# First pair of features of each FFN by eight plain products 512 wide, with the sums of blocks of x made beside it

## The chip, the cores and the metric

The kernel runs on 1 core of one Trainium2 chip. The metric is the device time of one execution in microseconds, the median of the runs shown; lower is better.

## What is computed

Two layers, each an FFN, a mixer and a second FFN, over 512 tokens (S) of 1024 features (DM). The change lies in the FFN alone; it runs four times (ffn1 and ffn2 of two layers).

```python
def rms_norm(x, w):
    xf = x.astype(jnp.float32)
    y = xf * lax.rsqrt(jnp.mean(xf * xf, axis=-1, keepdims=True) + NORM_EPS)
    return (y * w.astype(jnp.float32)).astype(x.dtype)

def swiglu_ffn(x, w_gate, w_up, w_down):
    return (jax.nn.silu(x @ w_gate) * (x @ w_up)) @ w_down

    for l in range(DEPTH):
        x = x + 0.5 * swiglu_ffn(rms_norm(x, ffn1_norm_w[l]), ffn1_w_gate[l], ffn1_w_up[l], ffn1_w_down[l])
        x = x + hybrid_mixer(rms_norm(x, mix_norm_w[l]), l, ...)
        x = x + 0.5 * swiglu_ffn(rms_norm(x, ffn2_norm_w[l]), ffn2_w_gate[l], ffn2_w_up[l], ffn2_w_down[l])
```

D_FF is 2816: 22 blocks of 128 features, worked on as 11 pairs (p = 0 to 10).

## The kernel before, in words

x lies in SBUF as eight tiles `x0` to `x7`, [128 features, 512 tokens] each. All arithmetic is fp32. A product of two fp32 operands is made of three matmuls: each operand is split into a rounded part (hi) and the rest (lo), and `mm3` (L114) issues hi·hi (L115), hi·lo (L116 or L117, by which operand has the lo part) and lo·hi. For weights `split` (L105) makes `whi` on ScalarE (L110) and `wlo` on VectorE (L111).

**Pairs.** `gate_up(p)` (L310) makes gate and up (s = 0, 1) of two feature blocks for all tokens. It sees weights and x as 2 x 2 block matrices (two feature blocks by odd and even input blocks; left and right half of the tokens, 256 each) and uses seven products of blocks and sums of blocks in place of eight. `STEPS` names the seven, in their order:

```python
    STEPS = (("11", 0, "X"), ("s1", 3, "Y"), ("s2", 4, "X"), ("s4", 2, "Y"), ("s3", 5, "X"), ("12", 1, "Z"), ("22", 6, "X"))
```

A product is 2 (s) x 4 (k) x 3 matmuls, 256 wide: 168 for a pair. Weights of a step are one tile [128, 1024], 512 KB. "11", "12", "21" and "22" are blocks as they lie in memory; s1 = 21 + 22, s2 = 11 - s1 with VectorE (L324), s4 = 12 + s2, s3 = 11 - 21. In most pairs s1 and s4 are made by accumulating DMAs on POOL's queue (L239, L326). A "plain" pair, p = 0 of each FFN and p = 1 of the first FFN, instead loads four `raw` blocks and makes s1 and s4 on VectorE too (L319). `raw` tiles (four buffers, shared with all other weights) are loaded by `load` (L98, L103), `rx` tiles (six buffers) by `loadx` (L223); both loads are on SP's queue, which takes them in order and stands where a buffer isn't free. The seven products are added into `c` by ScalarE and VectorE (L342 to L350), `c` is multiplied by the row `rsb` of 1/rms (L356), and silu(gate)·up is split into `hh`, `hl`.

**x for an FFN.** The blocks and sums of blocks of x, with their lo parts (`xR0` to `xR2`, `xT`), are made before the FFN begins: by `prep7` (L143) each time two tiles of x are finished, in w_out of the mixer (L1009) or in the last part of `down` (L374), and by `prep_all` (L249) at the start of the first FFN. `prep` (L129), which makes plain `xh`, `xl` of a tile, serves the mixer only. Squares of x are added into `sqacc` (L126). For the FFN `rms` (L302) multiplies `sqacc` by a matrix of ones (512 wide, L306) after the fifth product of pair 0, and `rstd` works on the 128x512 result; for the mixer `rms_of_x` (L187) makes four columns by eight one-column matmuls (L190), `rstd` works on 128x4, and `spread` (L195) makes the row.

**Order.** The instructions are written for one engine after the other as the code runs; a scheduler interleaves them by priority (`tc.high_priority()` puts loads and splits as early as buffers allow) and each engine then works strictly in its order. `after(n)` (L386) puts side work behind product n of a pair: rms, the bias row of the attention (`build_bias`, L416, in pair 1 of the first FFN: a load, two matmuls L426 through the single `side` bank, two copies L427, a store) and pieces of `down`.

## Time and profile before

| | us |
|---|---|
| median of 3 runs | 2014.24 (2011.62 to 2016.08) |
| the profiled execution | 2018.65 |
| its span | 2016.5 |

The profile and the trace are of one execution. Engines: PE is TensorE (PEld its weight loads), DVE VectorE, ACT ScalarE, POOL GpSimd, SP the engine that issues most DMAs (SPq its queue). L115 is line 115 of the kernel. Busy times are sums over an engine's instructions; an instruction that waits isn't busy. Matmuls overlap one another, so the step from start to start, and not the length of one, tells how fast they follow; VectorE's instructions overlap a little too. In brackets at the end of a row of the timeline stands how long the engine was idle before it and what released it. Consecutive like instructions stand in one row, with "x3" for three of them. PEclk is the TensorE clock that was granted, 1.00 being full speed.

### The profile page before, as it was taken

How to read it: one execution, taken by the hardware profiler on the slowest of the kernel's cores; microseconds unless marked ns; L12 is line 12 of the kernel's file. 1: busy time of each engine (PE TensorE's matmuls, PEld its weight loads, DVE VectorE, ACT ScalarE, POOL GpSimd, SP SyncE). 2: the span in 40 equal slices, each digit the busy share in tenths (PEclk: the TensorE clock that was granted, in tenths of full speed). 3: DMA queues.
4: the chain of work that ended last, by engine and by line, in shares of the span. 5: the costliest groups of instructions: out<-in, count | busy, mean ns of one | idle time of the engine just before them, and what ended most of it. 6: DMA issues, size and time to landing. Idle time of an engine off the chain costs nothing. (4 is left out here: it accounts for less than half of the span.)

```text
span 2016.5 us, 32318 instructions
## 1 busy us (share of the span) xinstructions
PE 1941.6 (96%) x12766; PEld 1761.9 (87%) x12766; DVE 1446.8 (72%) x2207; ACT 991.9 (49%) x1732; POOL 117.5 (6%) x173
## 2 busy tenths in 40 slices
PE   5899999999999899999989999999999988999999
PEld 5799999888878799999879999998898778999997
DVE  7876675769667697667679676657787687867665
ACT  6444443546545454444455454435466454545442
POOL 0100000011000000000000000000200000000000
PEclk8899999999989999999989999999999999999999
DMA  3766652445432675654257656525554127665622
GB/s 137 234 174 178 168 146 74 143 141 155 119 83 68 181 219 154 178 154 124 71 162 198 184 162 170 139 66 153 158 146 128 51 69 234 186 176 158 176 79 84
DMA packets 100099, 291.50 MB, mean 145 GB/s; under 512 B 10647, under 2 KB 23223, under 8 KB 99948
## 3 DMA queue, kind: packets, MB, share of 16 engines
q1 hardware_dynamic: 81900, 228.29, 34.5%
q0 software_dynamic: 18048, 61.15, 15.7%
q8 instruction: 100, 1.64, 0.3%
q14 instruction: 51, 0.42, 0.1%
HBM read 256.31 MB, written 7.66 MB: 131 GB/s over the span
## 5 line engine op out<-in xcount | busy, mean ns | idle before, releaser
L110 ACT CAST whi<-raw 128x1024 fp32r<-128x1024 f32 (+3 forms) x293 | 269.8, 921 | 443.2 <-PE side L116 221.5
L111 DVE TENSOR_TENSOR wlo<-raw,whi 128x1024 fp32r<-128x1024 f32 (+3 forms) x293 | 311.4, 1063 | 119.7 <-ACT whi L110 118.6
L115 PE MATMUL acc<-xT,whi 128*128 128x256 f32 x816 | 232.8, 285 | 0.8 <-ACT c L344 0.5
L116 PE MATMUL acc<-xT,whi 128*128 128x256 f32 x816 | 231.8, 284 | 0.0
L117 PE MATMUL acc<-xT,wlo 128*128 128x256 f32 x816 | 230.9, 284 | 0.1
L115 PE MATMUL side<-hh,whi 128*128 128x512 f32 x576 | 229.2, 398 | 0.0
L117 PE MATMUL side<-hh,wlo 128*128 128x512 f32 x576 | 226.9, 394 | 0.0
L116 PE MATMUL side<-hl,whi 128*128 128x512 f32 x576 | 225.8, 392 | 0.0
L117 PE MATMUL aux<-xR,wlo 128*128 128x256 f32 x704 | 201.3, 286 | 9.9 <-DVE wlo L111 9.9
L115 PE MATMUL aux<-xR,whi 128*128 128x256 f32 x704 | 203.0, 288 | 7.1 <-ACT whi L110 7.1
L116 PE MATMUL aux<-xR,whi 128*128 128x256 f32 x704 | 201.0, 285 | 0.0
L110 ACT CAST whi<-rx 128x1024 fp32r<-128x1024 f32 x117 | 122.6, 1048 | 140.1 <-PE aux L116 71.3
L111 DVE TENSOR_TENSOR wlo<-rx,whi 128x1024 fp32r<-128x1024 f32 x117 | 143.1, 1223 | 61.4 <-ACT whi L110 61.4
L115 PEld LDWEIGHTS acc<-xT,whi 128*128 128x128 f32 x816 | 157.8, 193 | 4.8 <-ACT c L344 1.6
L374 DVE TENSOR_TENSOR x<-side,x 128x512 f32<-128x512 f32 x96 | 66.3, 690 | 132.5 <-PE side L117 132.4
L111 DVE TENSOR_TENSOR wlo<-s,whi 128x1024 fp32r<-128x1024 f32 x98 | 119.4, 1223 | 58.4 <-ACT whi L110 58.1
L116 PEld LDWEIGHTS acc<-xT,whi 128*128 128x128 f32 x816 | 157.7, 193 | 2.0
L117 PEld LDWEIGHTS acc<-xT,wlo 128*128 128x128 f32 x816 | 156.6, 192 | 0.5 <-DVE wlo L111 0.5
L117 PEld LDWEIGHTS aux<-xR,wlo 128*128 128x128 f32 x704 | 136.7, 194 | 10.6 <-DVE wlo L111 10.6
L115 PEld LDWEIGHTS aux<-xR,whi 128*128 128x128 f32 x704 | 137.0, 195 | 9.9 <-ACT whi L110 7.3
L110 ACT CAST whi<-s 128x1024 fp32r<-128x1024 f32 x98 | 102.5, 1048 | 76.5 <-PE acc L116 26.7
L116 PEld LDWEIGHTS aux<-xR,whi 128*128 128x128 f32 x704 | 137.1, 195 | 2.0 <-issue 1.0
(351 smaller groups left out, 5037.2 us busy)
## 6 DMA issues: line engine op xcount, KB each, us to landing
rx<-wgu SPq DMA_DIRECT2D x156, 512.0 KB, 4.7
raw<-wgu SPq DMA_DIRECT2D x98, 512.0 KB, 4.6
raw<-wd SPq DMA_DIRECT2D x96, 384.0 KB, 3.3
rx<-wgu POOLq DMA_DIRECT2D x39, 512.0 KB, 7.6
rx<-s POOLq DMA_DIRECT2D x39, 512.0 KB, 6.4
raw<-win SPq DMA_DIRECT2D x24, 512.0 KB, 4.6
raw<-winf SPq DMA_DIRECT2D x24, 512.0 KB, 3.6
raw<-wd SPq DMA_DIRECT2D x32, 256.0 KB, 2.7
```

What stands on the lines that cost most here:

```text
L110: act.copy(hi[:, :n], raw[:, lo:lo + n])
L111: eng.tensor_tensor(lw[:, :n], raw[:, lo:lo + n], hi[:, :n].bitcast(F32), ALU.subtract)
L115: pe.matmul(out, lh, rh, start=first, stop=False, skip_group_check=skip)
L116: pe.matmul(out, lh, rl, start=False, stop=False, skip_group_check=skip)
L117: pe.matmul(out, ll, rh, start=False, stop=last, skip_group_check=skip)
L374: dve.tensor_tensor(x[d], ps, x[d], ALU.add)
```

## The change

Pair 0 of each FFN is no longer made by seven products of sums but by `gate_up0`: its four weight blocks times plain `xh`, `xl`, 2 x 4 x 3 matmuls for each, 96 in all, 512 wide. The first two blocks come as `raw`, the last two as `rx`. Its results are multiplied out of PSUM by `rsb` (four VectorE operations, 512 wide). So x is handed to each FFN as to the mixer, by `prep` for one tile at a time (with the first FFN the tiles come even ones first, behind two blocks of weights), and `prep7` and `prep_all` are gone. The sums of blocks of x are made behind the products of pair 0 (`sums(0)` to `sums(2)`) and behind the first product of pair 1 (`last_sum`), 256 wide, into three tiles and into parts of `xh`, `xl` that pair 0 has done with. rms goes through four columns behind product 0 and is spread behind product 2. Pair 1 of the first FFN is made like the later pairs, with accumulating DMAs. The bias row's inputs are loaded in pair 0, its matmuls come in pair 2 (before, pair 1), and its copies to 128 partitions in pairs 5 to 8 (before, 3 to 6).

```diff
-    def prep7(i, wcol, tmp, four):
...
-    def sums(t, b, out, eng):
...
-        def plain(p):
-            return p == 0 or first and p == 1
...
-            if plain(p):
-                return {b: load(w[n], soon) for n, b in ((0, "11"), (2, "21"), (3, "22"), (1, "12"))
-                        if not (first and p == 0 and n == 0)}
-            r = {"11": loadx(w[0]), "s1": loadx(w[2])}
-
-            with tc.high_priority():
+            r = {"11": loadx(w[0], soon), "s1": loadx(w[2], soon)}
+
+            with tc.high_priority() if soon else nullcontext():
                 pool.dma_start(out=r["s1"], in_=w[3], accum_op=ALU.add)
-            r["21"] = loadx(w[2])
-            r["s4"] = loadx(w[1])
-            r["12"] = load(w[1])
-            r["22"] = load(w[3])
+            r["21"] = loadx(w[2], soon)
+            r["s4"] = loadx(w[1], soon)
+            r["12"] = load(w[1], soon)
+            r["22"] = load(w[3], soon)
-        def prep_all():
...
+        raws0 = {}
         if first:
-                raws0 = {"11": load(aps["wgu"][l, which, 0, 0])}
-                for d in range(KD):
-                    nc.sync.dma_start(out=x[d], in_=aps["xT"][:, d, :])
+                for n in range(2):
+                    raws0[n] = load(aps["wgu"][l, which, 0, n])
+                    for d in range(n, KD, 2):
+                        nc.sync.dma_start(out=x[d], in_=aps["xT"][:, d, :])
                 nc.sync.dma_start(out=cn, in_=aps["cn"])
                 nc.sync.dma_start(out=bc, in_=aps["bc"])
-            prep_all()
-        xR, xT = parts["xR"], parts["xT"]
+            for d in range(KD):
+                prep(d, wcol, tmp)
+        xh, xl = parts["xh"], parts["xl"]
+        xT = [handed(4 + n, [P, 4, 2, 256], F32R, f"xT{n}") for n in range(3)]
+        neg = fp.tile([P, KD], F32, name="neg")
+        dve.tensor_scalar(neg, pv[:, wcol:wcol + KD], -1.0, None, ALU.mult)
+        t4 = fp.tile([P, 4, 256], F32, name="t4", tag="hh", bufs=HB)
+        left, right = slice(0, 256), slice(256, 512)
         hF = {}
...
         def x_of(f, k):
-            return xR[f][:, k] if f < 3 else xT[k][:, f - 3]
-        def rms():
-            ps = side()
-            tc.keep_in_program_order(pe.matmul(ps, ones, sqacc, start=True, stop=True))
-            rstd(rsb, DM, (tmp(), tmp()), ps)
+            if 3 <= f < 6:
+                return xT[f - 3][:, k, 0], xT[f - 3][:, k, 1]
+            d, t = ((2 * k, left), (2 * k + 1, left), (2 * k + 1, right), None, None, None, (2 * k, right))[f]
+            return xh[d][:, t], xl[d][:, t]
+        def sums(n):
+            for i in range(4):
+                a, b = x[2 * i], x[2 * i + 1]
+                w0, w1 = pv[:, wcol + 2 * i:wcol + 2 * i + 1], pv[:, wcol + 2 * i + 1:wcol + 2 * i + 2]
+                n0, n1 = neg[:, 2 * i:2 * i + 1], neg[:, 2 * i + 1:2 * i + 2]
+                if n == 0:
+                    d0 = fp.tile([P, 2, 256], F32, name="d0", tag="sn", bufs=4)[:, 0]
+                    dve.tensor_tensor(d0, a[:, right], a[:, left], ALU.subtract)
+                    act.activation(t4[:, i], d0, AF.Copy, scale=w0)
+                    v = t4[:, i]
+                elif n == 1:
+                    dve.scalar_tensor_tensor(t4[:, i], b[:, right], n1, t4[:, i], ALU.mult, ALU.add)
+                    v = t4[:, i]
+                else:
+                    v = fp.tile([P, 2, 256], F32, name="t3", tag="sn", bufs=4)[:, 0]
+                    act.activation(v, b[:, right], AF.Copy, scale=w1)
+                    dve.scalar_tensor_tensor(v, a[:, right], n0, v, ALU.mult, ALU.add)
+                hi, lo = xT[n][:, i, 0], xT[n][:, i, 1]
+                act.copy(hi, v)
+                dve.tensor_tensor(lo, v, hi.bitcast(F32), ALU.subtract)
+        def last_sum():
+            for i in range(4):
+                w1 = pv[:, wcol + 2 * i + 1:wcol + 2 * i + 2]
+                dve.scalar_tensor_tensor(t4[:, i], x[2 * i + 1][:, left], w1, t4[:, i], ALU.mult, ALU.add)
+                hi, lo = x_of(6, i)
+                act.copy(hi, t4[:, i])
+                dve.tensor_tensor(lo, t4[:, i], hi.bitcast(F32), ALU.subtract)
+        rst = {}
+        def gate_up0(after):
+            w = aps["wgu"][l, which, 0]
+            c = cbig("c")
+            ps = {}
+            for n in range(4):
+                m, par = divmod(n, 2)
+                raw = raws0[n] if n in raws0 else (load if n < 2 else loadx)(w[n], not first)
+                hi, lw = split(raw, 0, 1024)
+                for s in range(2):
+                    if par == 0:
+                        ps[s, m] = aux() if m else acc()
+                    for k in range(4):
+                        cc = slice(s * 512 + k * P, s * 512 + (k + 1) * P)
+                        d = 2 * k + par
+                        mm3(ps[s, m], hi[:, cc], lw[:, cc], xh[d], xl[d], d == 0, d == KD - 1)
+                after(n)
+            for m in range(2):
+                for s in range(2):
+                    dve.tensor_tensor(c[:, s, 2 * m:2 * m + 2].rearrange("p a b -> p (a b)"), ps[s, m], rsb, ALU.mult)
+            silu_gate(0, c)
...
-                if name not in raws and name != "s2" and name != "s3":
...
-                    dve.tensor_tensor(raws[name], raws[a], raws[b], ALU.add)
...
-                elif nxt[0] == "mx":
+                else:
                     prep(d, nxt[1], tmp)
-                elif d % 2:
-                    prep7(d // 2, nxt[1], tmp, four)
-        todo = []
+        todo, bias = [], []
         for p in range(KF // 2):
             when = WHEN[p < 9]
             base = 7 * (p % 3)
             def after(n):
-                if p == 0 and n == 4:
-                    rms()
-                if first and p == 1 and n == 2:
-                    build_bias(lambda name: cbig(name).rearrange("p a b c -> p (a b c)"))
-                if first and p in (3, 4, 5, 6) and n == 1:
-                    spread_bias(p - 3)
+                if p == 0:
+                    if n == 0:
+                        with tc.high_priority():
+                            rst["t"] = rms_of_x()
+                    if n == 2:
+                        spread(rst["t"])
+                    if n < 3:
+                        sums(n)
+                    if first and n == 3:
+                        bias.append(load_bias(lambda tag: fp.tile([P, WPC], F32, name="b" + tag, tag=tag, bufs=HB)))
+                    return
+                if p == 1 and n == 0:
+                    last_sum()
+                if first and p == 2 and n == 3:
+                    build_bias(*bias[0])
+                if first and p in (5, 6, 7, 8) and n == 1:
+                    spread_bias(p - 5)
                 for _ in range(when.count(base + n)):
                     if todo:
                         down(*todo.pop(0), side())
-            gate_up(p, after)
+            gate_up(p, after) if p else gate_up0(after)
...
-    def build_bias(big):
-        oh = big("oh")[0:33, 0:NREL]
+    def load_bias(big):
+        oh = big("hh")[0:33, 0:NREL]
         nc.sync.dma_start(out=oh, in_=aps["oh"])
         rb = tp.tile([33, 4], F32, name="rb")
         dve.memset(rb, NEG)
         nc.sync.dma_start(out=rb[0:32], in_=aps["rel_bias"])
         dve.tensor_scalar(rb, rb, -1.0, None, ALU.mult)
-        row = big("brow")[0:4, 0:NREL]
+        return oh, rb, big("hl")[0:4, 0:NREL]
+
+    def build_bias(oh, rb, row):
```

The order of SP's queue from w_out's last weights of the first mixer on, into the second FFN of layer 0 (`raw` of `wgu` and `rx` are weights of pairs 0, 1 and 2). Before, where `raw_6672` to `raw_6678` are pair 0's blocks, `raw_6941` and `raw_6943` pair 1's "12" and "22", and the four `rx` behind them the rest of pair 1:

```order
L103 DMA raw_6613<-wout 128x1024
L103 DMA raw_6672<-wgu 128x1024
L103 DMA raw_6674<-wgu 128x1024
L103 DMA raw_6676<-wgu 128x1024
L103 DMA raw_6678<-wgu 128x1024
L103 DMA raw_6941<-wgu 128x1024
L103 DMA raw_6943<-wgu 128x1024
L223 DMA rx_6932<-wgu 128x1024
L223 DMA rx_6934<-wgu 128x1024
L223 DMA rx_6937<-wgu 128x1024
L223 DMA rx_6939<-wgu 128x1024
```

Now, where `raw_6530`, `raw_6602`, `rx_6644` and `rx_6702` are pair 0's four blocks, `raw_6751` and `raw_6753` pair 1's "12" and "22", `raw_7010` and `raw_7012` pair 2's, and `rx_6742` and what follows it the rest of pair 1:

```order
L103 DMA raw_6482<-wout 128x1024
L103 DMA raw_6530<-wgu 128x1024
L103 DMA raw_6602<-wgu 128x1024
L103 DMA raw_6751<-wgu 128x1024
L103 DMA raw_6753<-wgu 128x1024
L103 DMA raw_7010<-wgu 128x1024
L103 DMA raw_7012<-wgu 128x1024
L190 DMA rx_6644<-wgu 128x1024
L190 DMA rx_6702<-wgu 128x1024
L190 DMA rx_6742<-wgu 128x1024
L190 DMA rx_6744<-wgu 128x1024
```

Pair 0 has two blocks fewer in the line of `raw` loads; its other two and pair 1's four follow as `rx` behind pair 2's two `raw` loads.

VectorE's order at the same place. Before, from x7's add on, up to the second product's weights (`s1`, `s2`, `s3` are sums of weight blocks of pair 0, `xt` and `xT` sums of blocks of x6 and x7):

```order
L1009 TENSOR_TENSOR x7_91<-aux_6619,x7_91 128x512
L167 TENSOR_TENSOR xt_6655<-xt_6655,xw_6646 128x256
L168 TENSOR_TENSOR xt_6655<-xw_6646 128x256
L169 TENSOR_TENSOR xt_6655<-xw_6646,xt_6655 128x256
L158 TENSOR_TENSOR xR1_6384<-xw_6646,xR1_6384 128x256
L158 TENSOR_TENSOR xR2_6385<-xw_6646,xR2_6385 128x256
L126 TENSOR_TENSOR sqacc_92<-sqacc_92,sq_6665 128x512
L171 TENSOR_TENSOR xT_6645<-xt_6655,xT_6645 128x4x256
L319 TENSOR_TENSOR s1_6714<-raw_6674,raw_6676 128x1024
L324 TENSOR_TENSOR s2_6749<-raw_6672,s1_6714 128x1024
L324 TENSOR_TENSOR s3_6814<-raw_6672,raw_6674 128x1024
L111 TENSOR_TENSOR wlo_6717<-s1_6714,whi_6716 128x1024
```

Now, from x7's add (L994) on, of which `xl4` is the lo part, `t4` and `xT0` a sum of blocks of x and its lo part, `rs_v` and `rs_q` steps of the four columns of rms; `wlo_6605`, the lo part of pair 0's second block, stands three rows ahead of this piece:

```order
L994 TENSOR_TENSOR x7_91<-aux_6488,x7_91 128x512
L140 SCALAR_TENSOR_TENSOR xl4_6402<-x7_91,pv_94,xh4_6401 128x512
L126 TENSOR_TENSOR sqacc_92<-sqacc_92,sq_6516 128x512
L222 TENSOR_SCALAR neg_6526<-pv_94 128x8
L244 TENSOR_TENSOR d0_6582<-x0_84 128x256
L162 COPY rst_6567<-aux_6562 128x4
L244 TENSOR_TENSOR d0_6587<-x2_86 128x256
L150 TENSOR_SCALAR rs_v_6569<-rst_6567 128x4
L244 TENSOR_TENSOR d0_6592<-x4_88 128x256
L151 TENSOR_SCALAR rst_6567<-rs_v_6569 128x4
L244 TENSOR_TENSOR d0_6597<-x6_90 128x256
L153 TENSOR_TENSOR rs_q_6570<-rst_6567 128x4
```

Ahead of pair 0's products now stand no sums of weights, and the sums of x come behind its first product, between the steps of rms.

## Rows read from the trace of the kernel before

**Rows 1.** The page, first part: busy time, share and instructions of each engine.

```profile
PE 1941.6 (96%) x12766; PEld 1761.9 (87%) x12766; DVE 1446.8 (72%) x2207; ACT 991.9 (49%) x1732; POOL 117.5 (6%) x173
```

**Rows 2.** Windows: length, busy of five engines (x instructions), PEclk, DMA share, GB/s.

```profile
7.05:88.06 81.01, 58.61 (x367) 54.17 (x368) 67.85 (x107) 44.83 (x83) 5.05 (x8) 0.83 0.52 171
659.10:718.01 58.91, 48.51 (x363) 46.37 (x362) 45.20 (x55) 28.63 (x45) 4.38 (x5) 0.94 0.71 207
1019.56:1083.82 64.26, 50.53 (x363) 48.35 (x362) 49.68 (x65) 30.23 (x50) 4.36 (x5) 0.87 0.65 187
1651.36:1710.88 59.52, 48.88 (x364) 46.59 (x362) 45.20 (x55) 28.61 (x45) 4.39 (x5) 0.94 0.68 202
650.00:659.00 9.00, 9.00 (x40) 7.26 (x39) 5.75 (x12) 3.28 (x7) 0.00 (x0) 1.00 0.00 0
```

**Rows 3.** Waits of PE, 7.05 to 88.06: us in total, times, longest.

```profile
PE aux L115 <- ACT whi L110: 12.3, 2, 7.1
PE acc L115 <- ACT xR L265: 7.4, 2, 7.0
PE side L426 <- DVE brow L427: 4.9, 1, 4.9
```

**Rows 4.** Waits of PE, 659.10 to 718.01, same columns.

```profile
PE aux L115 <- ACT whi L110: 4.4, 1, 4.4
PE aux L117 <- DVE wlo L111: 3.0, 1, 3.0
```

**Rows 5.** Timeline of PE: start, length, what, [idle before it <-releaser].

```profile
657.70 0.40 PE L115 MATMUL aux<-yh,whi 128*128 128x512 f32 x1
...
659.10 0.28 PE L115 MATMUL acc<-xR,whi 128*128 128x256 f32 x1
...
661.86 0.28 PE L117 MATMUL acc<-xR,wlo 128*128 128x256 f32 x1
666.55 0.58 PE L115 MATMUL aux<-xT,whi 128*128 128x256 f32 x1 [4.42 <-ACT whi L110]
...
670.03 0.41 PE L115 MATMUL aux<-xT,whi 128*128 128x256 f32 x1
...
672.59 0.34 PE L117 MATMUL aux<-xT,wlo 128*128 128x256 f32 x1
```

**Rows 6.** Timeline of DVE, same columns.

```profile
659.30 0.69 DVE L1009 TENSOR_TENSOR x<-aux,x 128x512 f32<-128x512 f32 x1 [2.15 <-PE aux L117]
...
661.46 0.42 DVE L169 TENSOR_TENSOR xt<-xw,xt 128x256 f32<-128x256 f32 x1
661.80 0.75 DVE L158 TENSOR_TENSOR xR<-xw,xR 128x256 fp32r<-128x256 f32 x2
...
686.11 2.36 DVE L324 TENSOR_TENSOR s<-rx 128x1024 f32<-128x1024 f32 x2 [5.33 <-DMA rx<-wgu]
...
699.28 1.23 DVE L324 TENSOR_TENSOR s<-rx 128x1024 f32<-128x1024 f32 x1 [3.40 <-DMA rx<-wgu]
```

**Rows 7.** Timeline of SP's queue of DMA issues.

```profile
644.80 23.89 SPq L103 DMA_DIRECT2D raw<-wgu  x3
668.85 4.06 SPq L223 DMA_DIRECT2D rx<-wgu  x5
```

**Rows 8.** Mixer's rms: timeline of PE, and instructions on `rst` (ns min/median/max).

```profile
395.64 0.95 PE L190 MATMUL aux<-ones,sqacc 128*128 128x1 f32 x8
...
402.58 1.05 PE L199 MATMUL aux<-cn,rst 128*128 128x128 f32 x8
...
L183 DVE TENSOR_TENSOR rs_q<-rst x6: 155/163/165, 397.2 to 1396.1; 128x4 f32<-128x4 f32 x6
```

**Rows 9.** The page, sixth part: DMA issues, KB each, us to landing.

```profile
rx<-wgu SPq DMA_DIRECT2D x156, 512.0 KB, 4.7
...
rx<-wgu POOLq DMA_DIRECT2D x39, 512.0 KB, 7.6
```

**Rows 10.** Timeline of ACT at the start of the program.

```profile
7.56 0.51 ACT L265 ACTIVATE xR<-x,pv 128x256 fp32r<-128x256 f32 x1 [0.56 <-DMA x<-xT]
```

More of the change, by code (lines that the diff above doesn't have):

```diff
@@ L141, in prep, with rstd @@
         square(d, tmp)
-    def prep7(i, wcol, tmp, four):
-        if i == 0:
-            parts["xR"] = [handed(4 + n, [P, 4, 2, 256], F32R, f"xR{n}") for n in range(3)]
-            parts["xT"] = []
-        xT = handed(i, [P, 4, 2, 256], F32R, "xT")
-        parts["xT"].append(xT)
-        xw = four("xw")
-        for n in range(2):
-            w = pv[:, wcol + 2 * i + n:wcol + 2 * i + n + 1]
-            act.activation(xw[:, 2 * n:2 * n + 2].rearrange("p a b -> p (a b)"), x[2 * i + n], AF.Copy, scale=w)
-        for n, b in enumerate((0, 2, 3)):
-            r = parts["xR"][n][:, i]
-            act.copy(r[:, 0], xw[:, b])
-            dve.tensor_tensor(r[:, 1], xw[:, b], r[:, 0].bitcast(F32), ALU.subtract)
-        sums(four("xt"), xw, xT, dve)
-        for n in range(2):
-            square(2 * i + n, tmp)
-    def sums(t, b, out, eng):
-        eng.tensor_tensor(t[:, 0], b[:, 1], b[:, 0], ALU.subtract)
-        eng.tensor_tensor(t[:, 1], t[:, 0], b[:, 3], ALU.subtract)
-        eng.tensor_tensor(t[:, 2], b[:, 3], b[:, 1], ALU.subtract)
-        eng.tensor_tensor(t[:, 3], b[:, 2], t[:, 1], ALU.add)
-        act.copy(out[:, :, 0], t)
-        dve.tensor_tensor(out[:, :, 1], t, out[:, :, 0].bitcast(F32), ALU.subtract)
-    def rstd(ssq, n, vq=None, src=None):
+    def rstd(ssq, n):
         shape = list(ssq.shape)
@@ L178, in rstd @@
             w *= m
-        v, q = vq or (tp.tile(shape, F32, name="rs_v", tag="rs_v%d" % w), tp.tile(shape, F32, name="rs_q", tag="rs_q%d" % w))
-        dve.tensor_scalar(v, ssq if src is None else src, 1.0 / n, EPS, ALU.mult, ALU.add)
+        v, q = (tp.tile(shape, F32, name="rs_v", tag="rs_v%d" % w), tp.tile(shape, F32, name="rs_q", tag="rs_q%d" % w))
+        dve.tensor_scalar(v, ssq, 1.0 / n, EPS, ALU.mult, ALU.add)
         dve.tensor_scalar(ssq.bitcast(I32), v.bitcast(I32), -0.5, float(0x5F3759DF), ALU.mult, ALU.add)
@@ L212, in cbig @@
             return fp.tile([P, 2, 4, 256], F32, name=name, tag="c", bufs=CB)
-        def four(name):
-            return cbig(name)[:, 0]
         def tmp():
@@ L309, in gate_up @@
         def gate_up(p, after):
             raws = blocks_of(p)
-            if first and p == 0:
-                raws["11"] = raws0["11"]
             c = cbig("c")
@@ L324, in gate_up @@
                         dve.tensor_tensor(raws[name], a, b, ALU.subtract)
-                        if name == "s2" and "s4" in raws:
+                        if name == "s2":
                             pool.dma_start(out=raws["s4"], in_=raws["s2"], accum_op=ALU.add)
@@ L336, in gate_up @@
                         cc = slice(s * 512 + k * P, s * 512 + (k + 1) * P)
-                        r = x_of(f, k)
-                        mm3(out, hi[:, cc], lw[:, cc], r[:, 0], r[:, 1], new and k == 0, k == 3, True)
+                        mm3(out, hi[:, cc], lw[:, cc], *x_of(f, k), new and k == 0, k == 3, True)
                     if name in copies:
@@ L473, in tmp0 @@
             return tmp("sq", "t0")
-        def four(name):
-            return mp.tile([P, 1280], F32, name=name, tag="big", bufs=NBIG)[:, 0:1024].rearrange("p (a b) -> p a b", b=256)
         def big(name):
@@ L1011, in w_out @@
                     nc.sync.dma_start(out=aps["out"][:, d, :], in_=x[d])
-                elif nxt[0] == "mx":
+                else:
                     prep(d, nxt[1], tmp0)
-                elif d % 2:
-                    prep7(d // 2, nxt[1], tmp0, four)
         for d in range(2):
```

46 lines of the change are left out of this document (5 added, 41 removed).

## The prediction

> **What bounds the kernel now.** The page's first part says that TensorE is busy for 96% of the span and VectorE for 72% [rows 1], so over the whole program only less TensorE work or fewer TensorE stops can shorten it. That share is a mean. The view by windows [rows 2] looks at the stages that the change touches: a "stretch" runs from the first matmul of pair 0 of an FFN to the first matmul of pair 2 on a sum of blocks. There are four, A to D, 81.01, 58.91, 64.26 and 59.52 us long. In them TensorE is busy only 58.6, 48.5, 50.5 and 48.9 us, and at a mean granted clock of 0.83 to 0.94, although w_out's matmuls just ahead of B ran without a gap at 1.00. So here the kernel is not bound by TensorE. The waits of TensorE name what ends last: in A rounded weights, blocks of x and the bias row [rows 3], in B rounded weights alone, 4.4 and 3.0 us the longest [rows 4].
>
> The timeline of TensorE gives the prices [rows 5]. Six 512-wide matmuls from 657.70 to 659.10 are 0.233 us each; the 23 steps of 256-wide ones from 659.10 to 661.86 are 0.120 each. Then comes the stop of 4.42, and after it the clock stands at its lower level (1.2 GHz): from 670.03 to 672.59 twelve steps at 0.213. A stretch of before at the full clock would be 2 x 168 x 0.120 for pairs 0 and 1 and 24 x 0.120 for the first product of pair 2, 43.2 us; so A loses 37.8, B 15.7, C 21.1 and D 16.3 to waits and the lower clock.
>
> Why the weights are late shows on VectorE [rows 6]. Ahead of pair 0's second product stand the rest of x's sums, then s1 and s2 of pair 0, each 1024 wide; TensorE stands still while they run. Later VectorE itself is idle for 5.33 us and 3.40 us, both times until a DMA of pair 1's blocks lands. Those DMAs were late because SP's queue stood for 23.89 us (644.80 to 668.69) in front of a load into a `raw` buffer [rows 7], and pair 1's blocks were behind it.
>
> **The change, part by part.**
> *Products of pair 0.* 96 matmuls of 512 replace 168 of 256: 22.40 against 20.16 us, +2.24 per FFN, all on TensorE's path.
>
> *rms.* Eight one-column matmuls take 0.95 us and the spread 1.05 in the mixer, which has the same code, and a 128x4 operation on VectorE 0.16 [rows 8]. I add 2.0 us of TensorE per FFN and credit nothing for the ones product that goes. The new floor of a stretch at full clock is 22.40 + 2.0 + 20.16 + 2.88 = 47.4 us, 4.2 above the old one: without stops to remove, the change would cost some 17 us over four FFNs.
>
> *VectorE.* Queued instructions start closer together than they last: two 256-wide in 0.75 against 0.42 for one, a step of 0.33; two 1024-wide in 2.36 against 1.23, a step of 1.13 [rows 6]. For 512 wide (0.69 alone) I take 0.60, as much less; for 128x4 ones, each of which needs the one before it, 0.20, a little above their length. By the order a stretch like B then holds: the tail of x7, 3 x 0.60; sums, 32 x 0.33; rms, 12 x 0.20; c and silu of pair 0, 4 x 0.60 + 2 x 1.13; lo parts of weights, 11 x 1.13; s2 and s3 of pairs 1 and 2, 4 x 1.13; c of pair 1, 4 x 0.33 + 0.60 + 2 x 1.13. That is 41 us, 4 less than the 45.2 busy before [rows 2], and under the floor of 47.4. What matters more: nothing but one lo part stands between pair 0's loaded blocks and TensorE, and the 32 small operations are due only with pair 1, some 20 us later.
> The Trainium skill, "VectorE: DVE Perf Modes", section "The TRN2 errata", says that every such instruction pays a fixed cost, about (N+151)/0.96 ns for an fp32 add of N elements: a rule against cutting sums into 256-wide pieces. Its formula gives an estimate of 424 ns for 256, and the trace agrees for one alone (0.42); in a queue the trace's step is 0.33. By the rule the 32 pieces would be 13.6 us and VectorE's sum 44.
>
> *Loads.* Two of pair 0's four blocks go through `raw`, two through `rx`. By SP's order two loads fewer stand in `raw`'s line ahead of the first `rx` load, and the last of these waits for the lo part of pair 0's second block, which VectorE's order puts ahead of x7's add (659.30 before [rows 6]); I put the `rx` loads at 656 to 660, some 10 us earlier than the 668.85 of before [rows 7]. Six blocks, of 4.7 us each from issue to landing as the page has it [rows 9], and the accumulating DMA on POOL at 7.6, then land by about 680, when pair 1 starts (659 + 22). So the idle times of 5.33 and 3.40 should go.
>
> *B and D.* Floor 47.4 and 2.0 for what stays (the small rms matmuls wait some for x7's square): 49.4; B gains 9.5 and D 10.1. *C* follows an FFN; it was 5 us longer than B, and I leave it 2 us more than B: 51.4, gain 12.9.
>
> *A.* Now a second block of weights is queued ahead of x, and x comes even blocks first; x already kept ScalarE waiting at 7.56 [rows 10]. Bounds from the rows: at best no stops, 47.4; at worst the waits of [rows 3] for weights and x all stay, 47.4 + 19.7, and the lower clock too. The mean clock of 0.83 over 81 us means some 27 us at half clock. I take 8 us at half clock in pair 0's 512-wide stream, 8 x (1 - 0.233/0.427) = 3.6 (0.427 is an estimate, twice the row of 0.213), and 7.1 us of waits, the longest single row. *Bias row:* the same two matmuls and copies go behind pair 2's fourth product; one side buffer is still between them, so I keep 3 of the 4.9 us. A comes to 47.4 + 3.6 + 7.1 + 3 = 61, gain 20.
>
> *Sum.* 20 + 9.5 + 12.9 + 10.1 = 52.5. The profiled execution took 2018.65 us (0.2% above the median of 2014.24; 2.15 us lie outside its span), so it would be 1966; the median 1962.
>
> **Rivals.**
> *1. VectorE keeps its turns.* It works in order: in the first FFN s2 of pair 1, which needs the accumulating DMA, stands ahead of the pieces of the first sum; in the others the small rms steps stand among them. If one wait like 4.4 [rows 4] stays in each later FFN, with the 6.04 us at half clock behind it (666.55 to 672.59, costing 6.04 x (1 - 0.120/0.213) = 2.6), 7.0 take the place of my 2.0: B, C and D gain 4.5, 7.9 and 5.1, and A 7 less, 13: 30.5 in all, 1984. For it: VectorE is filled to 41 of 47.4. Against: pair 1 has 20 us of slack. Chance 0.20.
>
> *2. All stops go.* Each stretch at the floor; A with the 2.8 us that a start at half clock costs and 4.9 for the bias row: 25.9 + 11.5 + 16.9 + 12.1 = 66.4, 1948. For it: four loads are ready before they are needed. Against: x at the start cannot come sooner. Chance 0.08.
>
> *3. Slower: pair 0's 512-wide stream runs at the lower clock.* Two banks alternate, each half product waits for its lo part, and short stops came with the lower level before [rows 5]. At 0.427 each, 96 cost 18.6 us more per FFN, 74.5 in all: 1962 + 74.5 = 2036. It decides once over 0.7 of the stream (52.5 of 74.5) runs low in all four FFNs. Against: w_out's 512-wide matmuls, which also alternate banks, ran at 1.00 for 9 us [rows 2]. Chance 0.05.
> The Trainium skill, "TensorE: Matmul & The Clock Gate", section "A second HAM failure mode: psum-queue depth-cycling", reports a kernel of 512-wide matmuls that cycled through PSUM banks and whose clock swung between its two levels, from short idle times between groups; by that rule this rival would hold. The trace's stretch at 1.00 speaks against it here.
>
> *4. The loads don't come earlier.* If the lo part that frees the last `raw` buffer runs behind x7's work, SP stands to 668.7 as before. Pair 0's third block then lands at 668.9 + 4.7 = 673.6 and is due at 659.1 + 11.2 = 670.3, 3.3 late; pair 1's stay as late as they were, with VectorE's 5.33 + 3.40 idle, which TensorE now waits out, and 2.6 of half clock. These 14.6 in place of 2.0 take 12.6 from each gain: -3.1, 0.3, -2.5 and 7.4, 2 in all, 2012. Chance 0.05: here the change wouldn't do what its order says.
>
> **How the numbers follow.** Forecast 0.62 (1950 to 1978), rival 1 0.20, rival 2 0.08, rival 3 0.05, rival 4 0.05. The range takes in the forecast and rivals 1 and 2 with some room for rival 1: 1946 to 1988. Measurements of this kernel can tell about 0.2%, 4 us. Faster: the first three, 0.90. Rival 4 lies on the border: 0.03 of it is the same, 0.02 goes to slower with rival 3, 0.07.
>
> **What would show it.** Right: pair 0 of the second FFN as 96 matmuls at 0.233 spacing, clock near 1.00 and no wait over 1 us; B and D 49 to 51 us long, C 51, A near 58 with the bias row's 3 us behind it in pair 2; SP's first `rx` load before 661; VectorE without idle time until a DMA. Wrong: 0.43 spacing in pair 0 (rival 3); a wait for weights of pair 1 behind VectorE (rival 1); SP standing past 668 (rival 4). The forecast itself would be wrong if the stretches are as long as forecast and the time is not: then something outside them, such as the handing over between phases, has moved.

## The result, and the profile after

The changed kernel takes 1948.67 us (median of 4 runs, 1947.55 to 1952.15) against 2013.64 of the kernel before (now of 4 runs), a ratio of 0.968 with a 95% interval of 0.9663 to 0.9697. The forecast was 1962 in a range of 1946 to 1988. One execution of rms_ones at 6633.35 us and one of the kernel before at 7056.4 stand far outside all others and are left out of the ratios. The profiled execution took 1947.55 us with a span of 1945.8; its page, first part, where [rows 1] stood before:

```profile
PE 1923.2 (99%) x12534; PEld 1738.4 (89%) x12534; DVE 1394.0 (72%) x2193; ACT 972.5 (50%) x1704; POOL 118.8 (6%) x175
```

TensorE went from 96% to 99% busy. The windows view of the same four stretches (columns as in [rows 2]):

```profile
8.24:61.45 53.21, 50.60 (x304) 45.04 (x305) 49.75 (x89) 37.64 (x67) 4.51 (x5) 1.00 0.91 279
630.63:677.51 46.88, 46.88 (x305) 42.76 (x304) 41.55 (x77) 30.18 (x54) 4.37 (x5) 1.00 0.82 234
979.32:1026.39 47.07, 46.93 (x305) 42.85 (x304) 42.06 (x79) 29.15 (x53) 4.38 (x5) 1.00 0.84 246
1593.33:1640.21 46.88, 46.88 (x305) 42.76 (x304) 41.56 (x77) 30.18 (x54) 4.38 (x5) 1.00 0.82 237
```

A went from 81.01 to 53.21, B from 58.91 to 46.88, C from 64.26 to 47.07, D from 59.52 to 46.88: 69.7 us together, with the two spans 70.7 apart (the section on the prediction adds up what else moved). B and D have no gap at all. In place of the waits of [rows 3, 4], the waits of TensorE in A (us in total, times, longest) are

```profile
PE acc L115 <- ACT xh L139: 8.2, 1, 8.2
PE aux L115 <- DVE c L286: 1.5, 1, 1.5
PE acc L116 <- DVE xl L140: 1.2, 1, 1.2
```

and none in B. The 8.2 is the time before the first product, the 1.5 a wait for VectorE to take pair 0's results out of PSUM, and the 1.2 the only further wait for x. The timeline of TensorE in A and then in B:

```profile
8.24 1.22 PE L115 MATMUL acc<-xh,whi 128*128 128x512 f32 x2 [8.24 <-ACT xh L139]
10.62 0.79 PE L116 MATMUL acc<-xl,whi 128*128 128x512 f32 x1 [1.15 <-DVE xl L140]
11.21 0.63 PE L117 MATMUL acc<-xh,wlo 128*128 128x512 f32 x1
...
15.90 0.52 PE L117 MATMUL acc<-xh,wlo 128*128 128x512 f32 x1
16.26 0.40 PE L115 MATMUL acc<-xh,whi 128*128 128x512 f32 x1
...
642.67 0.39 PE L115 MATMUL aux<-xh,whi 128*128 128x512 f32 x1
...
648.11 1.05 PE L169 MATMUL aux<-cn,rst 128*128 128x128 f32 x8
648.92 0.48 PE L115 MATMUL aux<-xh,whi 128*128 128x512 f32 x1
```

Ahead of the first product TensorE was idle. At the start the 512-wide products run at the lower level until 16.2 (0.43 apart: 11.21, then 11.63), in B at 0.227 (24 from 642.67 to 648.11). The spread takes 0.81. The column of the granted clock doesn't show this start; it reads 1.00 for it:

```profile
8.24:16.26 8.02, 6.86 (x16) 4.95 (x17) 8.02 (x12) 7.50 (x13) 0.00 (x0) 1.00 1.04 392
```

In the kernel before it is the same: the 256-wide products of its first 6.7 us stand 0.21 apart (13.08, then 13.29), with 1.00 in the column. So at the start of the program the steps tell the level, and the column does not. SP, POOL and VectorE around B, where [rows 6, 7] stood before:

```profile
602.09 25.57 SPq L103 DMA_DIRECT2D raw<-wgu  x6
627.72 38.91 SPq L190 DMA_DIRECT2D rx<-wgu  x13
...
637.07 0.86 POOL L199 DMA_DIRECT2D rx<-wgu  x1 [59.38 <-DMA rx<-wgu]
...
646.29 2.36 DVE L298 TENSOR_TENSOR s<-rx 128x1024 f32<-128x1024 f32 x2
```

The first `rx` load is issued 2.9 us ahead of the stretch (before: 9.75 us into it); the accumulating DMA for pair 1's s1 follows at 637.07, and VectorE subtracts at 646.29 without waiting for it. Pair 1's first product starts at 654.48 and its s2 is due some 6 us after that.

### The profile page after: what moved, and what is told of

It is laid out like the page before. It is cut to its first block, busy times and chain, and to the rows that moved or that the text cites. A ratio compares the mean times of both kernels' runs of the same rounds, so it can differ in the third digit from the quotient of the medians.

```text
span 1945.8 us, 31800 instructions
## 1 busy us (share of the span) xinstructions
PE 1923.2 (99%) x12534; PEld 1738.4 (89%) x12534; DVE 1394.0 (72%) x2193; ACT 972.5 (50%) x1704; POOL 118.8 (6%) x175
## 4 chain that ended last, share of the span: by engine, by line
PE 70%; DMA 1%; DVE 1%; ACT 1%; issue 0%; DVEq 0%; POOLq 0%; ACTq 0%
PE acc L116 9%; PE acc L115 9%; PE acc L117 9%; PE aux L117 6%; PE aux L116 6%; PE aux L115 6%; PE side L117 5%; PE side L115 5%; PE side L116 5%; PE po L117 1%; PE po L116 1%; PE po L115 1%; PE aux L938 1%; PE aux L809 1%; PE po L926 1%; DMA rx<-wgu 1%
## 5 line engine op out<-in xcount | busy, mean ns | idle before, releaser
L110 ACT CAST whi<-raw 128x768 fp32r<-128x768 f32 (+3 forms) x288 | 264.9, 920 | 450.1 <-PE side L116 221.5
L111 DVE TENSOR_TENSOR wlo<-raw,whi 128x768 fp32r<-128x768 f32 (+3 forms) x288 | 305.3, 1060 | 111.3 <-ACT whi L110 110.0
L115 PE MATMUL acc<-xh,whi 128*128 128x256 f32 (+1 forms) x736 | 238.5, 324 | 8.2 <-ACT xh L139 8.2
L116 PE MATMUL acc<-xl,whi 128*128 128x256 f32 (+1 forms) x736 | 238.9, 325 | 1.2 <-DVE xl L140 1.2
L117 PE MATMUL acc<-xh,wlo 128*128 128x256 f32 (+1 forms) x736 | 238.2, 324 | 0.0
L115 PE MATMUL aux<-xh,whi 128*128 128x256 f32 (+1 forms) x704 | 206.4, 293 | 0.0
L117 PE MATMUL aux<-xh,wlo 128*128 128x256 f32 (+1 forms) x704 | 206.1, 293 | 0.1
L116 PE MATMUL aux<-xl,whi 128*128 128x256 f32 (+1 forms) x704 | 206.1, 293 | 0.0
L117 PEld LDWEIGHTS acc<-xh,wlo 128*128 128x128 f32 x736 | 141.1, 192 | 9.2
L116 PE MATMUL acc<-xT,whi 128*128 128x256 f32 x480 | 135.9, 283 | 0.0
```

Source lines behind the costliest of these rows:

```text
L110: act.copy(hi[:, :n], raw[:, lo:lo + n])
L111: eng.tensor_tensor(lw[:, :n], raw[:, lo:lo + n], hi[:, :n].bitcast(F32), ALU.subtract)
L115: pe.matmul(out, lh, rh, start=first, stop=False, skip_group_check=skip)
L116: pe.matmul(out, lh, rl, start=False, stop=False, skip_group_check=skip)
L117: pe.matmul(out, ll, rh, start=False, stop=last, skip_group_check=skip)
```

## Experiments

Two things blur totals of single runs. First, each of the two mixers, in which no instruction was changed, takes either 265 to 266 or 268 to 271 us, in the kernel before as in all others; see the last section. So parts are compared by the lengths of the FFNs, from the first matmul of pair 0 to the first of the next phase (for the fourth FFN to the last matmul), read from TensorE's timeline in the profiled execution. Where TensorE waits ahead of the first matmul of the second to fourth FFN, as in b_unplain for 4.69, 8.22 and 4.69 us, that wait is counted into the FFN that it precedes. Second, these are single executions; differences under 1 us say little. Each ratio is to executions of the kernel before that were taken beside that run.

| kernel | A | B | C | D | sum | mixers |
|---|---|---|---|---|---|---|
| before | 382.6 | 360.5 | 366.7 | 360.8 | 1470.5 | 269.5, 265.1 |
| after | 356.4 | 348.7 | 348.5 | 348.2 | 1401.8 | 266.0, 265.5 |
| after, rms_ones | 361.7 | 350.6 | 356.6 | 352.6 | 1421.4 | 270.3, 269.8 |
| after, raw4 | 358.7 | 353.9 | 350.3 | 352.4 | 1415.3 | 265.8, 265.1 |
| after, both | 362.0 | 354.5 | 357.3 | 354.8 | 1428.6 | 270.1, 268.8 |
| after, narrow | 355.2 | 349.9 | 349.3 | 349.3 | 1403.7 | 270.4, 269.4 |
| after, bias_early | 356.5 | 348.3 | 349.9 | 348.1 | 1402.8 | 269.6, 267.7 |
| after, p1plain | 365.2 | 348.7 | 353.7 | 348.1 | 1415.7 | 269.5, 265.7 |
| after, warm | 355.7 | 348.8 | 352.7 | 348.7 | 1405.9 | 265.6, 269.5 |
| after, start4 | 356.9 | 348.4 | 349.2 | 348.8 | 1403.2 | 270.5, 269.7 |
| before, b_rms4 | 373.8 | 362.6 | 364.6 | 363.3 | 1464.3 | 269.5, 270.0 |
| before, b_rx | 380.9 | 357.3 | 362.5 | 359.0 | 1459.7 | 269.8, 265.3 |
| before, both (bb_rms4_rx) | 372.3 | 362.7 | 364.4 | 364.2 | 1463.6 | 269.8, 271.2 |
| before, b_unplain | 383.2 | 365.1 | 362.4 | 363.3 | 1474.0 | 269.9, 265.8 |

### rms_ones: rms by the matrix of ones again

```diff
...
-                            rst["t"] = rms_of_x()
+                            ps1 = side()
+                            pe.matmul(ps1, ones, sqacc, start=True, stop=True)
+                            rstd(rsb, DM, (tmp(), tmp()), ps1)
...
-                        spread(rst["t"])
```

> The changed kernel with one part undone: rms again by one product with the matrix of ones behind pair 0's first product, and rstd on 128x512. Theory S (supply: pair 0 no longer needs sums of weights made on VectorE, and pair 1's blocks are loaded earlier; the rms form is incidental): TensorE loses two groups of 0.81 us and gains one product of about 0.85, 0.8 us less per FFN; VectorE works some 5 us more per stretch and still fits; 1944 to 1957 us. Rival V (VectorE had too much to do, and the four columns relieved it): stops come back in each stretch, 5 us or more per FFN, 1968 us or more.

1975.69 us, ratio to before 0.9803 (0.979 to 0.9817). Theory S had this as incidental and was wrong: the FFNs are 19.6 us longer (5.3, 1.9, 8.1 and 4.4), as rival V said. V's reason, too much work on VectorE, is only part of it. In C the timelines of VectorE, ScalarE and TensorE, in this order, read:

```profile
1022.47 1.23 DVE L298 TENSOR_TENSOR s<-rx 128x1024 f32<-128x1024 f32 x1 [4.14 <-DMA rx<-wgu]
1023.61 0.42 DVE L256 TENSOR_TENSOR xT<-t,xT 128x256 fp32r<-128x256 f32 x1
...
1024.12 0.37 ACT L313 COPY sn<-aux 128x256 f32<-128x256 f32 x1 [4.11 <-DVE xT L256]
...
1024.54 0.38 PE L115 MATMUL aux<-xh,whi 128*128 128x256 f32 x1 [2.57 <-ACT sn L313]
```

VectorE stands idle for 4.14 us before s2 of pair 2, which waits for an accumulating DMA. The last pieces of the sums of x, put behind it in VectorE's order by the longer rms, wait with it; ScalarE waits for one of those, and its copies out of PSUM, which TensorE needs, wait behind that. It is a chain of turns, as in rival 1 of the prediction. In D VectorE stands idle for 3.70 us ahead of the same subtraction, and TensorE then waits 1.87 for a lo part and 1.42 for `c`, which both come behind it in VectorE's order. In A it is the work itself: from pair 1's s2 to the end of TensorE's long stop VectorE is busy for 18.33 of 18.59 us (columns as in [rows 2]); ScalarE waits 4.22 us in them for a piece of a sum of x, and TensorE for ScalarE:

```profile
26.89:45.48 18.59, 12.95 (x75) 11.27 (x73) 18.33 (x30) 7.00 (x14) 2.63 (x3) 0.94 0.91 258
...
45.48 0.58 PE L115 MATMUL acc<-xT,whi 128*128 128x256 f32 x1 [5.64 <-ACT sn L313]
```

### raw4: all four blocks of pair 0 through raw buffers

```diff
-                raw = raws0[n] if n in raws0 else (load if n < 2 else loadx)(w[n], not first)
+                raw = raws0[n] if n in raws0 else load(w[n], not first)
```

> The changed kernel with pair 0's third and fourth block loaded through raw buffers, like the first two. SP then stands in the line of raw buffers until pair 0's third block is split, and pair 1's four rx loads are issued some 12 us later (about 640 in place of 628 in the second FFN). Theory S: they are still due only with pair 1, so B to D lose 0 to 3 us each; 1949 to 1960. If the lead of 12 us itself is what the gain hangs on: 8 us or more per FFN, 1980 or more. Rivals V (VectorE's work) and W (512-wide products as such): no change beyond 4 us.

1960.09 us (1959.55 to 1962.89), ratio 0.9729 (0.9714 to 0.9743); the FFNs 13.5 us longer. SP and VectorE in B:

```profile
604.35 31.17 SPq L103 DMA_DIRECT2D raw<-wgu  x7
635.62 1.82 SPq L190 DMA_DIRECT2D rx<-wgu  x4
...
652.99 2.36 DVE L298 TENSOR_TENSOR s<-rx 128x1024 f32<-128x1024 f32 x2 [6.78 <-issue]
```

The `rx` loads come 2.7 us into the stretch in place of 2.9 ahead of it: 5.6 us later, not the 12 that I had expected. VectorE then idles 6.78 us ahead of s2 with the sums of x behind it (the profile names no releaser; that it is the DMA is inferred from the order), TensorE stops three times (0.55, 0.90, 1.49) and its mean clock in the stretch is 0.97. The expectation of 0 to 3 us each for B to D was low in B and D (5.2, 1.8, 4.2), that for the total just missed; rivals V and W had no change beyond 4 us, and it is 11.

### both: these two at once

> The changed kernel with two parts undone at once: rms by the matrix of ones, and all four blocks of pair 0 through raw buffers. Alone they cost the four FFNs 19.6 and 13.5 us (sums of the FFNs' lengths in the trace; the mixers vary by some 4 us each for reasons of their own). If the two causes are apart: 33 us more in the FFNs, 1980 to 1990 in all. If late blocks make a full VectorE worse: 45 us or more in the FFNs, 1995 or more. If they cost the same stops twice: 20 to 25 us, 1970 to 1978.

1981.21 us (1978.87 to 1984.53), ratio 0.9839 (0.9822 to 0.9857). The FFNs are 26.8 us longer, between "twice the same stops" (20 to 25) and "apart" (33). With both undone the FFNs are still 42 us shorter than before; that is the part of all else in the change, the plain products, the later sums and pair 1 of the first FFN above all.

### bb_rms4_rx, b_rms4, b_rx: the same two parts added to the kernel before

```diff
...
+                    rst0[0] = rms_of_x()
...
+                    spread(rst0[0])
...
-                return {b: load(w[n], soon) for n, b in
+                return {b: (loadx if p == 0 and not first and b in ("12", "22") else load)(w[n], soon) for n, b in
```

> The kernel before with one part of the change alone: rms of x by four columns behind pair 0's fifth product, and spread behind its seventh. Theory S: VectorE has some 5 us less to do per stretch, but it was idle for 8.7 us in B already, and the stops for sums and late blocks stay: 2004 to 2018. Rival V: most of the 65 us, 1985 or less.

> The kernel before, where in FFNs two to four pair 0's blocks 12 and 22 are loaded through rx buffers, so that SP's queue gets to pair 1's loads earlier. It is the earlier loading alone, with the sums of weights still on VectorE. If late loads carried half of the stops: VectorE's idle times of 5.33 and 3.40 us go, B to D gain 4 to 8 us each, 1990 to 2002. If the sums on VectorE alone were the cause: within 4 us of the kernel before.

> The kernel before with the same two parts added at once, rms by four columns and pair 0's last two blocks through rx buffers (FFNs two to four), and still seven products of sums for pair 0, and sums of x ahead of it. Alone they took 6 and 11 us from the four FFNs. If the sums on VectorE ahead of pair 0's products are the larger part: 10 to 25 us less, 1990 to 2005. If a freer VectorE and earlier blocks were enough together: 1980 or less, and the plain products could be left out.

b_rms4: 2015.85 us, ratio 1.0011 (0.9997 to 1.0024). b_rx: 2010.45, ratio 0.9975 (0.9965 to 0.9985). Both: 2016.3, ratio 1.0002 (0.9986 to 1.0019). So in the old kernel the small rms is not most of the gain, as rival V had it, and "a freer VectorE and earlier blocks are enough" is out too. In b_rx B to D gain 3.2, 4.2 and 1.8 us, short of the 4 to 8 expected. The small rms helps the first FFN (A 8.7 us shorter), where VectorE was fullest; B and D come out 2.1 and 2.5 longer, with a new stop behind a copy of ScalarE's (the second row below). In all three the stop for pair 0's s1 stays, as the waits of TensorE in bb_rms4_rx over the whole run show:

```profile
PE aux L115 <- ACT whi L110: 27.4, 5, 7.1
PE po L115 <- ACT sn L340: 12.2, 2, 6.6
```

My 10 to 25 us for bb_rms4_rx were wrong: two parts that take 20 and 13.5 us out of the changed kernel's FFNs bring 7 there, and nothing in the whole time, where pair 0 itself still stops.

### b_unplain: seven products for pair 0, with accumulating DMAs

```diff
-            return p == 0 or first and p == 1
+            return first and p < 2
```

> The kernel before, where pair 0 of FFNs two to four is made like the later pairs: seven 256-wide products, s1 and s4 made by accumulating DMAs. It gives up two of the four sums on VectorE and loads through rx buffers, with no plain products. Theory S: the supply is most of it, B to D gain 5 to 12 us each, and A nothing: 1978 to 1999. Rival W (the plain 512-wide products are what counts): within 6 us of the kernel before.

2023.82 us (2022.77 to 2025.28), ratio 1.0049 (1.0032 to 1.0065): half a per cent slower, against both theories. The timeline of TensorE, two rows in pair 0 of B and the first products of C and D:

```profile
664.59 0.58 PE L115 MATMUL acc<-xR,whi 128*128 128x256 f32 x1 [4.69 <-ACT whi L110]
...
675.16 0.58 PE L115 MATMUL aux<-xT,whi 128*128 128x256 f32 x1 [4.68 <-ACT whi L110]
...
1033.19 0.58 PE L115 MATMUL acc<-xR,whi 128*128 128x256 f32 x1 [8.22 <-ACT whi L110]
...
1657.92 0.58 PE L115 MATMUL acc<-xR,whi 128*128 128x256 f32 x1 [4.69 <-ACT whi L110]
```

and of SP and POOL at B:

```profile
655.03 36.98 SPq L223 DMA_DIRECT2D rx<-wgu  x11
...
664.27 0.85 POOL L239 DMA_DIRECT2D rx<-wgu  x1 [58.66 <-DVE sqacc L126]
```

Taking the sums off VectorE does not do when the DMA takes their place: the first `rx` load is issued at 655.03, and TensorE waits once for the block, ahead of the first product, and once for its sum (accumulated from 664.27 on). C gained 4.3 us, but B lost 4.6 and D 2.5. This is what plain products are for: a pair that needs no sum at all covers the load and the accumulating DMA of the next.

### narrow: pair 0's products 256 wide

```diff
-                        mm3(ps[s, m], hi[:, cc], lw[:, cc], xh[d], xl[d], d == 0, d == KD - 1)
+                        for h in (left, right):
+                            mm3(ps[s, m][:, h], hi[:, cc], lw[:, cc], xh[d][:, h], xl[d][:, h],
+                                d == 0 and h is left, d == KD - 1 and h is right, True)
```

> The changed kernel with pair 0's eight plain products made of 256-wide matmuls, 192 in place of 96, same order of weights. Theory S: 192 x 0.120 = 23.0 against 96 x 0.2275 = 21.8 us, 1.2 us more per FFN, 1953 to 1955, no new stop, clock at 1.00. Rival W (it is the 512-wide matmuls that keep TensorE busy and its clock up): granted clock below 1.00 in pair 0 and stops, 1965 or more.

1959.62 us (1957.62 to 1961.5), ratio 0.9723 (0.9708 to 0.9738), 5 us above the expectation. But the FFNs are 1.9 us longer (B, C and D 1.2, 0.8 and 1.1, as reckoned); the rest of the profiled run's excess is the mixers, 8.3 (last section). Pair 0 in B has no gap and the full clock:

```profile
634.20:657.40 23.20, 23.20 (x194) 23.01 (x194) 21.41 (x52) 14.81 (x31) 2.65 (x3) 1.00 0.79 234
```

So rival W is out: the products' width is worth 1 us per FFN.

### p1plain: pair 1 of the first FFN with sums on VectorE

```diff
+            if first and p == 1:
+                return {b: load(w[n], soon) for n, b in ((0, "11"), (2, "21"), (3, "22"), (1, "12"))}
...
+                if name not in raws and name not in ("s2", "s3"):
+                    a, b = ("21", "22") if name == "s1" else ("12", "s2")
+                    raws[name] = fp.tile([P, WPC], F32, name=name, tag="rx", bufs=RX)
+                    dve.tensor_tensor(raws[name], raws[a], raws[b], ALU.add)
...
```

> The changed kernel where pair 1 of the first FFN is made as before: four raw blocks, s1 and s4 added on VectorE, no accumulating DMAs there. If A's gain lies partly in taking these two sums (2.3 us) off VectorE: A 2 to 6 us longer, 1951 to 1957. If they are covered: A within 1 us, or 1 to 2 us shorter, since VectorE's wait of 1.57 us for the accumulating DMA goes: 1946 to 1950.

1961.15 us (1960.29 to 1965.12), ratio 0.9742 (0.9726 to 0.9759). A is 8.9 us longer, more than the 2 to 6 expected. VectorE and then TensorE:

```profile
47.81 1.21 DVE L299 TENSOR_TENSOR s<-raw,s 128x1024 f32<-128x1024 f32 x1
...
50.15 0.58 PE L115 MATMUL aux<-xh,whi 128*128 128x256 f32 x1 [4.68 <-ACT whi L110]
```

s4's add comes in its turn at 47.81, TensorE stops for 4.68, and half clock follows. The scheduler also moved the bias row's first matmul up to just ahead of this stop, and its second waits 2.03 us at 79.51 for the copy of the first, so not all of the 8.9 is the sums'. C is 5.2 longer by a stop of 3.58 us at 1027.87, of the kind that warm shows below; this edit changes no instruction there.

### bias_early, warm, start4

bias_early: `if first and p == 1 and n == 2` for `p == 2 and n == 3`. warm: 16 matmuls `pe.matmul(warm[:, 0:P], ones, ones, ...)` ahead of all. start4: 22 of them, and

```diff
-                    raws0[n] = load(aps["wgu"][l, which, 0, n])
+                    raws0[n] = load(aps["wgu"][l, which, 0, n], n == 0)
...
-            for d in range(KD):
-                prep(d, wcol, tmp)
+            for d in (0, 2, 4, 6, 1, 3, 5, 7):
+                with tc.high_priority():
+                    prep(d, wcol, tmp)
...
+                    if first and i in (1, 2):
+                        tc.keep_in_program_order(ins)
```

> The changed kernel with the bias row's two matmuls back in pair 1 of the first FFN, behind its third product; its inputs are still loaded in pair 0. If the place mattered: TensorE waits 3 to 5 us for the first of the two copies on VectorE, as before the change, 1952 to 1955. If it was the fullness of VectorE in the old first FFN: no wait over 1 us, 1948 to 1950.

> The changed kernel with sixteen matmuls of the matrix of ones on itself, results unused, ahead of the first product, while TensorE waits for weights and x (0 to 8.24 us). If the half clock of the first 8 us of products follows from TensorE's idleness before: 0.227 us per matmul from the start, and up to 3.6 us less, less what x's arrival then takes back: 1945 to 1948. If x's arrival alone sets the pace there: 1948 to 1950.

> The changed kernel with another start: 22 matmuls of ones (results unused) until data comes, pair 0's second block of weights loaded behind the even tiles of x, x's lo parts ahead of the second block's on VectorE, and two of the small differences behind them. If the first FFN's start is bound by what stands ahead of the first lo part of x and by the clock: first product at about 7.0, no wait of 1.6 us behind it, full clock, and the first FFN ends 3 to 5 us earlier than at 364.6; 1944 to 1947. If x's arrival sets the pace: 1 us or less.

bias_early: 1951.27 us (1950.07 to 1954.66), ratio 0.968 (0.9667 to 0.9694); no wait at the bias row, and A as long as after the change. The scheduler put its two matmuls 8 us apart (47.50 and 55.51); in the changed kernel they stand at 70.18 and 73.64 with products between. So the edit alone doesn't put the place to the test. But the kernel before tells the cause:

```profile
60.31 0.70 PE L426 MATMUL side<-oh,rb 33*4 33x320 f32 x2
...
79.90 0.48 DVE L427 COPY brow<-side 4x320 f32<-4x320 f32 x1
...
80.44 1.22 PE L426 MATMUL side<-oh,rb 33*4 33x320 f32 x2 [4.87 <-DVE brow L427]
```

There the two matmuls stand 20 us apart. The second waits for the copy of the first, which VectorE comes to 19 us late, behind steps of rms and sums and lo parts of weights. In b_rms4 and bb_rms4_rx, where only rms is smaller on VectorE and the bias row is still in pair 1, the copies come at 64.3 and 62.9, and this wait is gone. So it was VectorE's full order in the old first FFN, the second theory.

warm: 1955.76 us (1955.48 to 1957.21), ratio 0.971 (0.9695 to 0.9724). The first FFN ends 0.4 us earlier only. The dummy matmuls ended at 6.4, 2.1 us ahead of the first product, and a wait of 1.64 for x's lo part followed; the clock was low again until 14.35. C lost 4.2 us, for this reason (VectorE and TensorE):

```profile
1011.75 1.23 DVE L301 TENSOR_TENSOR s<-rx 128x1024 f32<-128x1024 f32 x1 [3.90 <-DMA rx<-wgu]
...
1014.16 0.39 PE L120 MATMUL aux<-xh,wlo 128*128 128x256 f32 x1 [2.88 <-DVE wlo L114]
```

In the changed kernel's own profile the same subtraction starts 2 us earlier, and TensorE loses only 0.3 us (one step of 0.42 in place of 0.12, at 1011.71):

```profile
1009.72 1.22 DVE L298 TENSOR_TENSOR s<-rx 128x1024 f32<-128x1024 f32 x1 [3.20 <-DMA rx<-wgu]
```

C has no slack there: with the DMA 2 us later it loses 4 to 5.

start4: 1958.03 us (1957.02 to 1959.02), ratio 0.9723 (0.9709 to 0.9738). No gain; the first product starts at 8.11, not at 7.0, and the first FFN ends 0.4 us later. TensorE's timeline:

```profile
1.06 7.30 PE L97 MATMUL aux<-ones 128*128 128x128 f32 x44 [1.06 <-DVE rb L412]
8.11 0.71 PE L118 MATMUL acc<-xh,whi 128*128 128x512 f32 x2
...
18.96 0.39 PE L120 MATMUL acc<-xh,wlo 128*128 128x512 f32 x1
21.81 0.39 PE L118 MATMUL acc<-xh,whi 128*128 128x256 f32 x1 [2.46 <-ACT whi L113]
```

The first two blocks ran at full clock without a gap and were done at 19.2, where the changed kernel ended them at 23.9 (24.7 less the 0.8 of the small rms matmuls). So with a row of matmuls up to the first product the products run at full clock from the first on, and x's arrival doesn't set their pace. Then the scheduler had put pair 1's first product (256 wide) ahead of pair 0's third; it waits 2.46 us for its weights, and the clock fell again. Some 4 us may be had there, but no run here has them. No version ran faster than the changed kernel.

## Why the prediction was right, and where its terms were off

The direction, the place and the mechanism held; the size was 13 us short, and what came is by time and by description rival 2 (all stops go, 1948, chance 0.08), not the forecast. The range held because it was made to take in rival 2: by the forecast's own signs B and D should have been 49 to 51 us long and C 51, with VectorE nowhere idle until a DMA, and they were 46.9 and 47.1, with such a wait of 3.20 in C.

- **Pair 0 and rms** were sized a little high: 0.227 per 512-wide matmul and 0.81 for the spread gave a stretch of 46.9, not 47.4.
- **What stays in B, C and D** was 2.0, 4.0 and 2.0 us; it is 0, 0.2 and 0. The small rms matmuls met no wait. C follows an FFN and is not longer for that.
- **A** was the worst term: 58 and 3 for the bias row behind it, against 53.2 and none. I kept the 7.1 us of the longest row for weights and x. That was the wait at 37.28 for a sum of weights of pair 0 that VectorE made behind its sums of x, which is just what the change takes away; left are 1.2 for x and 1.5 for VectorE at the results of pair 0. The worst case of 19.7 us of waits was too high as well: 7.0 of the 7.4 for x in [rows 3] is TensorE's idle time ahead of its first product, outside the stretch. Half clock at the start was nearly right (3.6 reckoned; 16 matmuls at 0.427 in place of 0.227 are 3.2), but the 27 us at half clock that I read from the mean clock of before were too few, as the column misses the first 6.7 us. The 3 us of the bias row did not come: the one side buffer is still there, but VectorE now comes to the copy of the first matmul in time (72.53, the second matmul 73.64; see bias_early).
- **Loads** came as the order said: first `rx` load 2.9 us ahead of the stretch, within the 3 ahead to 1 behind that I gave. In B pair 1's sum by DMA was ready before VectorE's turn.
- **VectorE's sum** was 41 us in B; 41.55 is measured. But I credited the smaller rms with nothing of its own. Undoing it cost 19.6 us: in A by its work, in C and D (12.5) by what it pushed behind a waiting instruction as well. The latter is rival 1's mechanism, which the change as made escapes by a few us. C's 3.20 us idle for a DMA shows how few.
- **Rival 3** (lower clock in the 512-wide stream) did not come: 1.00 in B, C and D, with a step of 0.227, and in A the lower level only until 16.2, as at the start of the kernel before. The Trainium skill, "TensorE: Matmul & The Clock Gate", section "A second HAM failure mode: psum-queue depth-cycling", puts such a swing of the clock down to short idle times between groups of matmuls. In B and D this stream goes from bank to bank with no idle time at all, so its condition was not met here.
- **The 32 small pieces** came as reckoned. The Trainium skill, "VectorE: DVE Perf Modes", section "The TRN2 errata", has a fixed cost for every instruction; by an estimate from its formula VectorE's sum would have been 44. The trace agrees with it for one instruction alone (0.42) and not in a queue, where 41.55 us hold all 32.
- **Sum.** The stretches gave 69.7 where 52.5 was forecast. The start took 1.2 back (8.24 against 7.05) and the rest of the FFNs 1.0; the mixers gave 3.1, though no instruction of theirs was changed: the first one's clock fell in the profiled execution of before and not in that of after (last section). Medians differ by 65: the profiled execution of before lay 5 us above its median, that of after 1 us below.

What the runs show of the parts: in the old kernel neither rms nor the loads do it (-6 and -11 us in the FFNs, and -7 together), the width is worth 2, the loads 13.5 and rms 20 once pair 0 is plain (27 together), and 42 are left with those two undone. Not tried: the plain products with x's sums still ahead of pair 0, so how these 42 divide between the plain products and the later sums stays open, but for at most 9 us of pair 1 in the first FFN.

## What to carry to other kernels

Put a unit of work that needs nothing prepared at the head of a stage, so that its length covers the loads and sums of the next; it may cost more on the engine that bounds (here 3.7 us per FFN, 46.9 against 43.2) and still win. An engine that is 89% busy, as VectorE in B, and works in order should not have a wait for a DMA in front of work that others need; a little more work can push such a piece behind the wait. Judge parts by removing them from the finished version as well as by adding them to the old one: here two parts that took 7 us out of the FFNs of the old version cost 27 when taken out of the new one.

## What the runs showed of the hardware

The 512-wide steps differ with no change of form: 0.233 in w_out [rows 5] and 0.227 in most of pair 0 of the changed kernel, both at a granted clock of 1.00. Why is open.

At the start of the program the column of the granted clock reads 1.00 while steps of 0.43 (512 wide) and 0.21 (256 wide) show the lower level, before the change and after.

The mixers' two lengths come from one place, some 172 us into each, where TensorE waits up to 2 us, mostly for a tile of VectorE's; in some its clock falls there, for the same instructions. The windows view of the kernel before, first and second mixer:

```profile
561.00:575.00 14.00, 12.50 (x44) 9.48 (x45) 6.83 (x13) 8.26 (x29) 1.73 (x2) 0.63 0.46 118
1558.00:1572.00 14.00, 12.51 (x72) 10.11 (x73) 10.35 (x21) 10.40 (x35) 1.25 (x2) 1.00 0.42 104
```

0.63 and 1.00, 44 matmuls and 72. In the changed kernel's profile both are at 1.00, in narrow's both fall. So it is in the profiles of all fourteen kernels: a mixer is long where the clock falls there, and short where it stays at 1.00. It adds some 4 us per mixer. The change touches no instruction of a mixer, yet a kernel seems to keep its own pattern: the mean clock of each of narrow's four executions is 0.994 or 0.995, of the changed kernel's 1.000, 0.996, 1.000 and 0.999. So up to 8 us between the totals of two kernels can come from here; what decides it was not found.
